# Two-layer decoder trunk on one core: row pools opened amid the gate tiles, seven PSUM banks outside the scores, later spreads and stores, the root on ScalarE

## The chip, the core and the metric

The kernel runs on one core of a Trainium2 chip. TensorE does the matmuls, VectorE (DVE), ScalarE (ACT) and GpSimd (POOL) the elementwise work; each takes its instructions in the order in which they were written to it. SyncE (SP) issues all DMAs, also in order. The metric is the device time of one execution in microseconds; lower is better.

## What is computed

Two post-norm layers on 1024 tokens of width 1024. Layer A mixes with dilated sliding-window attention (three dilations, merged by their softmax denominators), layer B with windowed grouped-query attention with sinks. Cut to what matters here:

```
h = x @ w_in                                   # q, k, v and the gate columns z
o = merged or windowed attention of q, k, v
m = (o * silu(z)) @ w_out                      # output projection
x = layer_norm(ALPHA * x + m, ln_g, ln_b)
x = x + sigmoid(x @ w_gate) * (p @ w_proj)     # the second gate
```

## The kernel before

Every product runs on pairs of f16 numbers (high and low part): `lin` makes one 128x512 tile of a product with 24 matmuls (8 steps of the contraction, three products each). A layer is a chain of such tiles, 8 row tiles of 128 tokens for each block of 512 weight columns. Between the matmuls of a tile `sub_tick` puts attention units (scores, softmax, values) in, so that TensorE has work while they go on.

Weights come as a list of blocks. `weight_steps` is a generator that runs one step of it at a time: load a block by four DMAs, take four maxima on VectorE (`wpm`), put the maximum on a diagonal (`max_diag`, tile `mdd`), spread it over the partitions with one small TensorE matmul into a bank `s` (`max_spread`, `s<-mdd,ones`), make scales, and split each quarter into its high part (ScalarE) and low part (VectorE). `progress` and `prepare` advance it after each tile of a product by a number of steps that is given there.

After the attention of a layer come the gate tiles z (`z_block`, `z_tile`): two halves of 512 columns, 8 row tiles each. ScalarE reads the PSUM tile twice (`zt`, `zu`), VectorE joins them, SP stores them in DRAM (`za`, `zb`). Then `mixed` runs the output projection. `rows(n)` loads the mixed attention (`ot`) and the gate (`og`), multiplies them on GpSimd, takes the row maximum on ScalarE, splits the product (`rhl`) and transposes it by a DMA into `ogT`. `norm(n)` multiplies `ogT[n]` with both halves of the output weights (the blocks `whl` and `wo`), adds the residual `y`, normalises (`rsqrt`) and transposes the result into `xgT`, from which `gate` computes the second gate (blocks `whl` and `wg`). At the end of each layer's attention `drain` runs what is left of units and merges before the pools of the rows are opened. A scheduler of the framework sorts each engine's instructions once more when the program is built, so the order on an engine is not that of the code alone.

PSUM has eight banks: three for `lin`, four for `s`, one for `o`. Before the change all product tiles use the three of `lin`, except in the startup.

Of the kernel before, what the change touches and what calls it, by code (L numbers as in the profile page):

```python
# [20 lines left out]
P = 128  # L21
S = 1024
D = 1024
# [57 lines left out]
W_OP = 2  # L81
N_WAKE = 8
Z_AHEAD = 1
# [5 lines left out]
class Block:  # L89
# [14 lines left out]
    def maxima(self):  # L104
        k, q = self.k, self.n // 4
        pm = k.small.tile([P, 4], F32, tag="wpm", name="wpm")
        for c in range(4):
            k.nc.vector.tensor_reduce(pm[:, c:c + 1], self.raw[:, c * q:(c + 1) * q], axis=AX.X, op=ALU.max,  # L108
                                      apply_absolute_value=True)
            yield True  # L110
        diag = k.max_diag(pm)
        yield True
        e = k.max_spread(diag)
        self.s, self.inv = k.keep(1, "s"), k.keep(1, "inv")
        k.pow2_of(e, self.s, self.inv)
        yield True
# [22 lines left out]
class Trunk:  # L139
    def __init__(self, ctx, tc, a):  # L140
# [13 lines left out]
        self.uid = 0  # L154
# [25 lines left out]
        self.mhalf = self.const.tile([P, 1], F32, name="mhalf")  # L180
        nc.gpsimd.memset(self.mhalf, -0.5)
# [7 lines left out]
    def rope_tables(self, order):  # L189

        t = self.const.tile([P, N_ROPE], F32, name="rope", tag="rope", bufs=2)
# [124 lines left out]
    def drain(self):  # L316
        due, self.due = self.due, []
        for e in due:
            e[1]()
        while self.units or any(self.pipe):  # L320
            self.unit_step()
        self.merge_every = 1
        while self.merges or self.merging:
            self.merge_step()

# [9 lines left out]
    def rope_out(self, ps, nq, nk, n, dst):  # L335
# [6 lines left out]
        t2 = w.tile([P, 512], F32, tag="t2", name="t2")  # L342
# [8 lines left out]
        hl = w.tile([P, 12, P], F16, tag="hl", name="hl", bufs=3)  # L351
# [251 lines left out]
    def next_block(self):  # L603
        b = self.blocks[self.bi]
        self.bi += 1
        while not b.done:
            assert next(self.steps)
        return b
# [13 lines left out]
    def layer_a(self):  # L622
# [14 lines left out]
        for pair in range(2):  # L637
            for g in (1, 2, 0):
                self.rope_tables(g)
# [4 lines left out]
                for n in range(NT):  # L644
                    ps = self.ps_lin.tile([P, 512], F32, tag="lin", name="lin")
                    self.lin(ps, blk, *self.stat_a(g, n), 0, 512)
                    self.v_out(ps.rearrange("p (s c) -> p s c", s=2), vh[:, pick, n, :], vl[:, pick, n, :])
                    self.progress()
# [18 lines left out]
        self.z_block(self.invx, lambda n: self.stat_a(0, n))  # L667
        self.drain()
# [15 lines left out]
    def unit_a(self, q, g, n, qk, vh, vl, cs, ncs, cv, scr):  # L684
# [4 lines left out]
        def stats():  # L689
            st = at.tile([P, 4 * HD + 8], F32, tag="st", name="st", bufs=len(self.pipe) + 1)  # L690
            return st, st[:, 4 * HD:4 * HD + 4], st[:, 4 * HD + 4:]
# [20 lines left out]
    def z_rows(self, pool, ps, c):  # L712
# [4 lines left out]
        u = pool.tile([P, 512], F32, tag="t2", name="zu")  # L717
# [9 lines left out]
    def z_block(self, invx, stat):  # L727

        self.z_stat = stat
        self.upt = 2.0  # L730
        for half in range(2):
            self.w_z = self.next_block()
            self.cz = self.prod(invx, self.w_z.inv, 0.5, "cz")
            for n in range(Z_AHEAD if half else NT):
                self.z_tile(self.work, n, half)
                self.progress()
            if half == 0:
                self.w_z.released = True

    def merge(self, n, pair, scr):  # L740

        nc, at, sp = self.nc, self.att, self.small
# [44 lines left out]
    def layer_b(self, xT, invx):  # L787
# [42 lines left out]
        self.z_block(invx, lambda n: self.stat_t(xT, n))  # L830
        self.drain()
# [45 lines left out]
    def mixed(self, l, xres, gate_pool):  # L877
# [4 lines left out]
        g_b = pw.tile([P, D], F32, tag="g_b", name="g_b", bufs=1)  # L882
        b_b = pw.tile([P, D], F32, tag="b_b", name="b_b", bufs=1)
        nc.sync.dma_start(g_b, a["lng"][l].partition_broadcast(P))
        nc.sync.dma_start(b_b, a["lnb"][l].partition_broadcast(P))
# [3 lines left out]
        w_o, cw = [], []  # L889
# [17 lines left out]
        def norm(n):  # L907
            y = pw.tile([P, D], F32, tag="row", name="y", bufs=6)
            nc.sync.dma_start(y, xres(n))
            sc = sp.tile([P, 2], F32, tag="osc", name="osc")  # L910
            st = sp.tile([P, 2, 6], F32, tag="bst", name="bst")
            for hf in range(2):
                sl = slice(512 * hf, 512 * hf + 512)
                nc.vector.tensor_mul(sc[:, hf:hf + 1], ris[n], cw[hf])
                ps = self.ps_lin.tile([P, 512], F32, tag="lin", name="lin")
# [13 lines left out]

        done = 0  # L930
        for n in range(Z_AHEAD, NT):
            self.z_tile(self.work, n, 1)
            self.tick()
            self.prepare(5)
            if n >= NT - ROWS_AHEAD:
                rows(done)
                done += 1
        self.w_z.released = True
        for i in range(2):
            b = self.next_block()  # L940
            c = self.keep(1, "cw")
            nc.vector.tensor_scalar(c, b.inv, 1.0 / ALPHA, None, op0=ALU.mult)
            w_o.append(b)
            cw.append(c)
        for n in range(NT):
# [4 lines left out]
            if n == 1:  # L950
                wg = gate_pool()
        for b in w_o:
            b.released = True
        return xgT, xg_dr, wg

    def gate(self, l, xgT, xg_dr, last):

        nc, a, pw = self.nc, self.a, self.pw
        w_g = [self.next_block(), self.next_block()]
# [5 lines left out]
        for n in range(NT):  # L965
# [5 lines left out]
            for c0, c1 in ((0, 512), (512, 768), (768, 1024)) if end else ((0, 512), (512, 1024)):  # L971
                hf, sl, w = c0 // 512, slice(c0, c1), c1 - c0
                ps = self.ps_lin.tile([P, 512], F32, tag="lin", name="lin")[:, :w]
                self.lin(ps, w_g[hf], *self.stat_t(xgT, n), c0 % 512, w)
                t = pw.tile([P, 512], F32, tag=("g_b", "b_b")[hf], name="gth", bufs=1)[:, :w]
# [18 lines left out]
    def rsqrt(self, var):  # L994
# [5 lines left out]
        nc.gpsimd.tensor_tensor(r, v, self.mhalf, op=ALU.pow)  # L1000
# [6 lines left out]
    def build(self):  # L1007
# [39 lines left out]
        work, self.work = opened("work", 2)  # L1047
        lower.append(work)
        with tc.tile_pool(name="att", bufs=2) as self.att:
            self.layer_a()  # L1050
        tp, self.tp = opened("tp", 9, side="right")
        pw, self.pw = opened("pw", 2, side="right")

        def gate_pool(name):
# [3 lines left out]
            return p  # L1058

        xgT, xg_dr, wg = self.mixed(0, lambda n: a["x"][n * P:(n + 1) * P, :], lambda: gate_pool("wg"))  # L1060
        x2T, x2_dr = self.gate(0, xgT, xg_dr, False)
        close(wg)
        close(pw)
# [3 lines left out]
        with tc.tile_pool(name="kv", bufs=1) as self.kv, tc.tile_pool(name="att2", bufs=2) as self.att:  # L1067
            self.layer_b(x2T, self.x2_s[1])
        pw, self.pw = opened("pw2", 2, side="right")
        xgT, xg_dr, wg = self.mixed(1, lambda n: x2_dr[n], lambda: gate_pool("wg2"))  # L1070
        self.gate(1, xgT, xg_dr, True)
        close(wg)
        close(pw)
        close(tp)
# [69 lines left out]
```

## Time and profile before

| | us |
|---|---|
| median of 3 runs | 1663.25 (1661.86 to 1665.62) |
| profiled execution, own time | 1667.52 |
| its span on the core | 1665.7 |
| TensorE busy | 1592.0 |
| VectorE busy | 1085.1 |
| ScalarE busy | 923.8 |
| GpSimd busy | 677.8 |

The span is that of the profiled execution; about 2 us lie around it in its own time. TensorE is busy for most of the span, so the time is what TensorE needs, plus what it waits, plus what it loses while its clock is at the lower of its two levels. The mean granted clock was 0.984 of 2.4 GHz.

### The profile page before, as it was taken

What the parts mean: (1) busy time and instruction counts of PE and PEld (TensorE: products, weight loads), DVE (VectorE), ACT (ScalarE), POOL (GpSimd) and SP (SyncE); (2) the same over time, 40 slices, a digit from 0 to 9 for tenths busy, and PEclk for the clock granted to TensorE, in tenths of its full rate; (3) what the DMA queues carried; (4) which work ended last, traced back from release to release, by engine and by line L of the source; (5) the groups of instructions that cost most, each with busy time, mean ns of one, the idle gap of its engine ahead of it and who ended that gap; (6) DMA issues with size and microseconds to landing.
All of it is one profiled execution on the core that took longest, in us unless ns stands there. A gap on an engine that the chain in (4) does not pass through costs nothing. (4 is left out here: it accounts for less than half of the span.)

```text
span 1665.7 us, 29033 instructions
## 1 busy us (share of the span) xinstructions
PE 1592.0 (96%) x10579; PEld 883.1 (53%) x10579; DVE 1085.1 (65%) x2617; ACT 923.8 (55%) x2050; POOL 677.8 (41%) x481
## 2 busy tenths in 40 slices
PE   9899999999999799999999988899999998999998
PEld 3455676654555356666555543344455555544444
DVE  6766655655666876556556667887447998777731
ACT  4536764674765376656657843533334878754321
POOL 0205523432564666244235553453323452225341
PEclk9999999999999899999999999999999999999999
DMA  9618766774787768567648986989975898897963
GB/s 363 246 61 168 166 153 134 161 165 112 159 165 201 215 153 163 130 151 158 155 118 170 191 236 203 335 227 257 252 183 116 156 205 176 192 296 212 257 198 110
DMA packets 543792, 311.02 MB, mean 187 GB/s; under 512 B 473120, under 2 KB 494240, under 8 KB 543392
## 3 DMA queue, kind: packets, MB, share of 16 engines
q1 hardware_dynamic: 543648, 309.16, 75.0%
q8 instruction: 83, 1.36, 0.4%
q14 instruction: 61, 0.50, 0.1%
HBM read 137.78 MB, written 54.92 MB: 116 GB/s over the span
## 5 line engine op out<-in xcount | busy, mean ns | idle before, releaser
L270 PE MATMUL lin<-whl,xhl 128*128 128x512 f16 x1280 | 489.9, 383 | 0.0
L271 PE MATMUL lin<-whl,xhl 128*128 128x512 f16 x1280 | 489.2, 382 | 0.0
L272 PE MATMUL lin<-whl,xhl 128*128 128x512 f16 x1280 | 488.9, 382 | 0.0
L399 POOL TENSOR_TENSOR phl<-sm,phl 128x1024 f16<-128x1024 f32 (+1 forms) x88 | 155.1, 1763 | 234.6 <-ACT phl L397 213.0
L349 POOL TENSOR_TENSOR t<-t,t 128x512 f32<-128x512 f32 (+1 forms) x120 | 153.4, 1278 | 236.9 <-DVE t L348 219.9
L108 DVE TENSOR_REDUCE wpm<-wraw 128x1 f32<-128x1024 f32 (+1 forms) x132 | 157.2, 1198 | 99.3 <-DMA wraw<-in_wa_dram 57.2
L272 PEld LDWEIGHTS <-xhl 128*128 128x128 f16 x1280 | 149.6, 117 | 128.2 <-issue 4.6
L270 PEld LDWEIGHTS <-xhl 128*128 128x128 f16 x1280 | 149.5, 117 | 120.0 <-issue 4.3
L271 PEld LDWEIGHTS <-xhl 128*128 128x128 f16 x1280 | 149.8, 117 | 117.0 <-issue 4.0
L393 ACT ACTIVATE sm<-sm,st,cs 128x128 f32<-128x128 f32 (+1 forms) x384 | 203.6, 532 | 3.3
L356 POOL TENSOR_TENSOR hl<-t,hl 128x512 f16<-128x512 f32 (+1 forms) x120 | 146.0, 1217 | 133.0 <-ACT hl L355 133.0
L387 DVE CUSTOM_DVE_ANT_0 sm<-s,tab 128x256 f32<-128x256 f32 (+1 forms) x512 | 157.3, 359 | 34.0 <-PE s L383 28.9
L132 DVE SCALAR_TENSOR_TENSOR whl<-wraw,s,whl 128x1024 f16<-128x1024 f32 (+1 forms) x116 | 169.2, 1510 | 9.6 <-ACT whl L131 9.5
L355 ACT ACTIVATE hl<-t 128x512 f16<-128x512 f32 (+1 forms) x120 | 72.3, 603 | 121.9 <-POOL t L349 120.1
L345 DVE TENSOR_TENSOR t<-lin,rope 128x512 f32<-128x512 f32 (+1 forms) x120 | 79.0, 658 | 89.3 <-PE lin L272 64.5
L131 ACT ACTIVATE whl<-wraw,s 128x1024 f16<-128x1024 f32 (+1 forms) x116 | 121.8, 1123 | 7.0 <-DVE s L210 7.0
L270 PE MATMUL lin<-whl,x2T 128*128 128x512 f16 (+1 forms) x320 | 114.9, 359 | 0.0
L271 PE MATMUL lin<-whl,x2T 128*128 128x512 f16 (+1 forms) x320 | 114.7, 359 | 0.0
L272 PE MATMUL lin<-whl,x2T 128*128 128x512 f16 (+1 forms) x320 | 114.7, 359 | 0.0
L397 ACT ACTIVATE phl<-sm 128x1024 f16<-128x1024 f32 (+1 forms) x128 | 110.3, 862 | 1.3
L359 ACT ACTIVATE hl<-hl 128x512 f16<-128x512 f16 (+1 forms) x104 | 63.3, 608 | 56.5 <-POOL hl L356 56.2
L383 PE MATMUL s<-qk 128*128 128x128 f16 x1120 | 81.8, 221 | 9.9 <-DMA qk<-hl 9.9
(190 smaller groups left out, 2905.3 us busy)
## 6 DMA issues: line engine op xcount, KB each, us to landing
wraw<-in_wa_dram SPq DMA_DIRECT2D x56, 512.0 KB, 5.6
scr<-st SPq DMA_DIRECT2D x96, 132.0 KB, 2.3
gt<-scr SPq DMA_DIRECT2D x48, 264.0 KB, 3.5
wraw<-in_wav_dram SPq DMA_DIRECT2D x24, 512.0 KB, 6.4
prh<-pro SPq DMA_DIRECT2D x32, 256.0 KB, 4.2
wraw<-in_wg_dram SPq DMA_DIRECT2D x16, 512.0 KB, 8.8
wraw<-in_wb_dram SPq DMA_DIRECT2D x16, 512.0 KB, 6.4
xg<-y SPq DMA_DIRECT2D x16, 512.0 KB, 3.4
```

The costliest lines, as they stand in the source:

```text
L108: k.nc.vector.tensor_reduce(pm[:, c:c + 1], self.raw[:, c * q:(c + 1) * q], axis=AX.X, op=ALU.max, apply_absolute_value=True)
L131: nc.scalar.activation(hl[:, 0, sl], self.raw[:, sl], AF.Copy, scale=self.s)
L132: nc.vector.scalar_tensor_tensor(hl[:, 1, sl], self.raw[:, sl], self.s, hl[:, 0, sl], op0=ALU.mult, op1=ALU.subtract)
L270: mm(ps, xh(kt), wh, start=(kt == 0), stop=False)
L271: mm(ps, xh(kt), wl, start=False, stop=False)
L272: mm(ps, xl(kt), wh, start=False, stop=(kt == NK - 1))
L349: nc.gpsimd.tensor_add(t1[:, :nh * HD], t1[:, :nh * HD], t2[:, :nh * HD])
L356: nc.gpsimd.tensor_sub(hl[:, :nh, HD:P], rv, hl[:, :nh, 0:HD])
L387: nc.vector.tensor_tensor_reduce(sm[:, h, :nk], ps[:, i, :nk], mask, 1.0, -3e38, ALU.add, ALU.max, mx[:, h:h + 1])
L393: nc.scalar.activation(sm[:, h, :nk], sm[:, h, :nk], AF.Exp, bias=nbias[:, h:h + 1], scale=cs, accum_out=sums[:, h:h + 1])
L397: nc.scalar.activation(hl[:, 0], sm[:, :, :nk], AF.Copy)
L399: eng.tensor_sub(hl[:, 1], sm[:, :, :nk], hl[:, 0])
```

## The change

- **Pools.** The pools of the rows (`pw`, `tp`) open as soon as the last attention unit is through, amid the gate tiles of the first half (`gate_tiles`), not after all merges; `drain` is gone. What the merges need (`gt`, `st`) moves to a pool of its own, `attm`, and `hl` to `att`. The pool of the last gate block (`wg`) opens ahead of the output projection, and holds `g_b` and `b_b`, which are loaded there.
- **Banks.** `bank()` takes product tiles from `lin` and `s` in turn, seven banks in all, in the second half of z, the output projection and the second gate.
- **Spreads.** From the first gate tile to the second gate, the spread of a weight block's maximum comes two tiles of TensorE work after its diagonal.
- **Stores and steps.** A gate tile is stored after the next one is written; `zu` has three buffers. The numbers of weight steps change: 3 a tile in both halves of z (before: 1.6 and 5) and 1 a tile in the output projection (before: 2).
- **Root.** The inverse root of the variance is a square root on ScalarE and a reciprocal on VectorE, not a power on GpSimd.
- **Rope.** One buffer instead of two, loaded at the third tile of the block that precedes its use.

```diff
 W_STEPS = 1.6
-W_OP = 2
+SPREAD = 2.0
+W_OP = 1
-Z_AHEAD = 1
+W_GATE = 3
...
         diag = k.max_diag(pm)
         yield True
+        at = k.work_done + SPREAD
+        while k.work_done < at and k.late:
+            yield False
         e = k.max_spread(diag)
...
+    def bank(self):
+        self.turn += 1
+        pool, tag = ((self.ps_s, "s"), (self.ps_lin, "lin"))[self.turn % 7 % 2]
+        return pool.tile([P, 512], F32, tag=tag, name=tag)
...
     def z_tile(self, pool, n, half):
-        ps = self.ps_lin.tile([P, 512], F32, tag="lin", name="lin")
+        ps = self.bank() if half else self.ps_lin.tile([P, 512], F32, tag="lin", name="lin")
         self.lin(ps, self.w_z, *self.z_stat(n), 0, 512)
-        self.nc.sync.dma_start(self.z_dr[n][:, 512 * half:512 * half + 512], self.z_rows(pool, ps, self.cz))
+        out = self.z_out
+        self.z_out = (self.z_dr[n][:, 512 * half:512 * half + 512], self.z_rows(pool, ps, self.cz))
+        for o in (out, self.z_out if half and n == NT - 1 else None):
+            if o:
+                self.nc.sync.dma_start(*o)
...
+    def gate_tiles(self, leave):
+        self.upt = 2.0
+        self.late = True
+        self.z_block(0)
+        for n in range(NT):
+            self.z_tile(self.work, n, 0)
+            self.progress(W_GATE)
+            if leave and not (self.due or self.units or any(self.pipe)):
+                leave()
+                leave = None
...
+        self.z_block(1)
         done = 0
-        for n in range(Z_AHEAD, NT):
+        for n in range(NT):
             self.z_tile(self.work, n, 1)
             self.tick()
-            self.prepare(5)
+            self.prepare(W_GATE)
             if n >= NT - ROWS_AHEAD:
                 rows(done)
                 done += 1
+        while self.merges or self.merging:
+            self.merge_step()
+        gp = gate_pool()
+        g_b = gp.tile([P, D], F32, tag="g_b", name="g_b", bufs=1)
+        b_b = gp.tile([P, D], F32, tag="b_b", name="b_b", bufs=1)
...
         for n in range(NT):
             norm(n)
...
-            if n == 1:
-                wg = gate_pool()
...
         r = sp.tile([P, 1], F32, tag="rr", name="rr")
-        nc.gpsimd.tensor_tensor(r, v, self.mhalf, op=ALU.pow)
+        nc.scalar.activation(r, v, AF.Sqrt)
+        nc.vector.reciprocal(r, r)
```

The first place is TensorE where the gate tiles of layer A end (`xhl` is the layer's input, `ogT` the transposed row of the output projection). Before:

```order
L271 MATMUL lin<-whl,xhl 128x512
L272 LDWEIGHTS xhl
L272 MATMUL lin<-whl,xhl 128x512
L235 LDWEIGHTS ones
L235 MATMUL s<-mdd,ones 128x128
L270 LDWEIGHTS ogT
L270 MATMUL lin<-whl,ogT 128x512
```

In the changed kernel there:

```order
L275 MATMUL lin<-whl,xhl 128x512
L276 LDWEIGHTS xhl
L276 MATMUL lin<-whl,xhl 128x512
L274 LDWEIGHTS ogT
L274 MATMUL s<-whl,ogT 128x512
```

The spread between the last gate tile and the first tile of the output projection is gone, and that tile goes to a bank of `s`. After the last value matmul of the attention both kernels have 10 gate tiles to go. Before, four spreads stand behind 1, 5, 7 and 10 of them; in the changed kernel the first two stand behind 0 and 8, the third behind the fourth tile of the output projection, and the fourth between its last tile and the first tile of the second gate.

The second place is SP's queue ahead of the first rows in layer A (`za_609`, `oa_601` and so on are row tiles in DRAM, numbered on by one; `lng`, `lnb` the weights of the normalisation). Before:

```order
L725 DMA za_611<-zu 128x512
L884 DMA g_b<-in_lng_dram 128x1024
L885 DMA b_b<-in_lnb_dram 128x1024
L894 DMA ot<-oa_601 128x1024
L895 DMA og<-za_609 128x1024
L894 DMA ot<-oa_602 128x1024
L895 DMA og<-za_610 128x1024
```

In the changed kernel (row tile 0 is `za_610` and `oa_602` here):

```order
L731 DMA za_610<-zu 128x512
L103 DMA wraw<-in_wg_dram 128x1024 x2
L905 DMA og<-za_610 128x1024
L904 DMA ot<-oa_603 128x1024
L731 DMA za_611<-zu 128x512
L782 DMA oa_608<-gt 128x2x256
L782 DMA oa_609<-gt 128x2x256
L731 DMA za_612<-zu 128x512
L905 DMA og<-za_611 128x1024
L904 DMA ot<-oa_604 128x1024
L905 DMA og<-za_612 128x1024
```

The first row's loads move ahead of the last two merges' stores; those of the second and third row stay behind them and behind the store of the third gate tile. `g_b` and `b_b` move down, behind the loads of the last weight block.

The third place is VectorE, layer A, ahead of the low parts of the second half of the output weights (`wo`; `m<-s` reads what the spread made). Before:

```order
L237 TENSOR_REDUCE m_11746<-s 128x1
L766 TENSOR_TENSOR gt<-gt 128x2x256
L719 SCALAR_TENSOR_TENSOR zu<-zt,zu 128x512
L216 TENSOR_REDUCE m_11833<-wpm 128x1
L209 TENSOR_SCALAR inv_11749<-m_11746 128x1
L224 TENSOR_SCALAR mdt<-m_11833 128x1
L210 RECIPROCAL s_11748<-inv_11749 128x1
L942 TENSOR_SCALAR cw_12028<-inv_11749 128x1
L226 TENSOR_SCALAR mde<-mdt 128x1
L228 TENSOR_SCALAR mdd<-tab,mde 128x128
L132 SCALAR_TENSOR_TENSOR wo<-wraw,s_11748,wo 128x1024 x4
```

In the changed kernel, from the third row on (`p2t<-rm` is the first step on a row's maximum):

```order
L205 TENSOR_SCALAR p2t<-rm 128x1
L207 TENSOR_SCALAR p2e<-p2t 128x1
L213 TENSOR_SCALAR ri<-p2e 128x1
L214 RECIPROCAL rs<-ri 128x1
L241 TENSOR_REDUCE m_11857<-s 128x1
L213 TENSOR_SCALAR inv_11860<-m_11857 128x1
L214 RECIPROCAL s_11859<-inv_11860 128x1
L954 TENSOR_SCALAR cw_11580<-inv_11860 128x1
L266 SCALAR_TENSOR_TENSOR rhl<-og,rs,rhl 128x1024
L921 TENSOR_SCALAR osc<-cw_11580,ri 128x2 x2
L721 SCALAR_TENSOR_TENSOR zu<-zt,zu 128x512
L136 SCALAR_TENSOR_TENSOR wo<-wraw,s_11859,wo 128x1024 x4
```

The scale of `wo` now stands behind the maxima of three rows, where before no row stood ahead of it. ScalarE has four more table loads: in each layer one ahead of the first row's square root and one behind the last, ahead of the second gate's first tanh.

## Rows read from the trace of the kernel before

**Rows 1.** The page, busy time: engine, us, share of the span, instructions.

```profile
PE 1592.0 (96%) x10579; PEld 883.1 (53%) x10579; DVE 1085.1 (65%) x2617; ACT 923.8 (55%) x2050; POOL 677.8 (41%) x481
```

**Rows 2.** What TensorE waited for: us in total, times, longest us.

```profile
PE s L235 <- DVE mdd L228: 21.9, 4, 7.4
PE s L383 <- DMA qk<-hl: 9.9, 6, 4.0
PE o L414 <- ACT st L694: 8.7, 4, 4.9
PE o L414 <- DVE mu L858: 8.7, 6, 2.7
PE o L414 <- DMA pT<-phl: 8.6, 5, 4.7
```

**Rows 3.** Timeline of TensorE, layer A: start, us, instruction, [idle before it].

```profile
992.59 0.19 PE L416 MATMUL o<-vh,pT 128*128 128x64 f16 x1
...
995.21 0.38 PE L270 MATMUL lin<-whl,xhl 128*128 128x512 f16 x1
...
995.86 0.38 PE L270 MATMUL lin<-whl,xhl 128*128 128x512 f16 x1
...
1035.32 0.29 PE L235 MATMUL s<-mdd,ones 128*128 128x128 bf16 x1 [6.17 <-DVE mdd L228]
...
1061.33 0.29 PE L235 MATMUL s<-mdd,ones 128*128 128x128 bf16 x1 [7.44 <-DVE mdd L228]
...
1061.89 0.59 PE L270 MATMUL lin<-whl,ogT 128*128 128x512 f16 x1 [0.27 <-PE s L235]
...
1118.68 0.39 PE L270 MATMUL lin<-whl,ogT 128*128 128x512 f16 x1 [2.94 <-DMA ogT<-rhl]
...
1154.47 0.38 PE L270 MATMUL lin<-whl,xgT 128*128 128x512 f16 x1
```

**Rows 4.** The same for layer B, where its gate tiles end.

```profile
1492.71 0.29 PE L235 MATMUL s<-mdd,ones 128*128 128x128 bf16 x1 [3.32 <-DVE mdd L228]
```

**Rows 5.** Windows: stretch, length, busy us of PE, PEld, DVE, ACT, POOL, clock, DMA.

```profile
1060.00:1065.00 5.00, 3.40 (x9) 1.26 (x10) 4.51 (x12) 4.44 (x6) 0.00 (x0) 0.51 0.99 225
1061.90:1154.50 92.60, 86.85 (x387) 38.30 (x388) 77.39 (x159) 32.32 (x36) 42.26 (x24) 0.97 0.95 254
1492.80:1578.50 85.70, 85.70 (x386) 38.37 (x387) 65.05 (x122) 32.10 (x35) 39.13 (x22) 0.97 0.90 238
```

**Rows 6.** Timeline of VectorE, ScalarE and SP, layer A, weights and first row.

```profile
1019.28 1.53 SPq L102 DMA_DIRECT2D wraw<-in_wg_dram  x2
...
1024.69 1.22 DVE L108 TENSOR_REDUCE wpm<-wraw 128x1 f32<-128x1024 f32 x1 [1.55 <-DMA wraw<-in_wg_dram]
...
1034.53 0.33 SPq L725 DMA_DIRECT2D za<-zu  x1
...
1034.98 0.29 DVE L228 TENSOR_SCALAR mdd<-tab,mde 128x128 bf16<-128x128 f32 x1
...
1036.33 4.26 ACT L131 ACTIVATE wo<-wraw,s 128x1024 f16<-128x1024 f32 x4 [9.02 <-DMA oa<-gt]
...
1037.57 1.01 SPq L895 DMA_DIRECT2D og<-za  x1
...
1048.90 0.15 DVE L201 TENSOR_SCALAR p2t<-rm 128x1 f32<-128x1 f32 x1 [4.61 <-ACT ot L900]
...
1052.55 4.89 SPq L874 DMA_TRANSPOSE ogT<-rhl  x1
```

**Rows 7.** Tile ogT, 1036 to 1170: from issue to landing.

```profile
DMA to landing us min/median/max: 4.3/4.7/7.5
```

**Rows 8.** VectorE, layer A, the evacuation of the output projection.

```profile
1126.09 1.41 DVE L917 SCALAR_TENSOR_TENSOR y<-lin,osc,y 128x512 f32<-128x512 f32 x2 [4.00 <-DMA y<-in_x_dram]
```

**Rows 9.** Groups: busy us, mean ns, idle before: the root, the table load, low parts.

```profile
L1000 POOL TENSOR_TENSOR rr<-rv,mhalf 128x1 f32<-128x1 f32 x16 | 22.5, 1403 | 61.7 <-DVE rv L998 50.9 <-DMA wraw<-in_wb_dram 7.8 <-DVE rs L210 3.1
...
L486 ACT ACT_TABLE_LOAD x1 | 1.3, 1283 | 0.7 <-PEq L1133 0.7
...
L132 DVE SCALAR_TENSOR_TENSOR whl<-wraw,s,whl 128x1024 f16<-128x1024 f32 (+1 forms) x116 | 169.2, 1510 | 9.6 <-ACT whl L131 9.5
```

More of the change, by code (lines that the diff above doesn't have):

```diff
@@ L153, in __init__ @@
         self.o_i = 0
-        self.uid = 0
+        self.uid = self.turn = 0
+        self.z_out = None
+        self.late = False
         self.bufs = 2
@@ L189, in rope_tables @@
     def rope_tables(self, order):
-        t = self.const.tile([P, N_ROPE], F32, name="rope", tag="rope", bufs=2)
+        t = self.const.tile([P, N_ROPE], F32, name="rope", tag="rope")
         self.nc.sync.dma_start(t, self.a["tab"][:, order * N_ROPE:(order + 1) * N_ROPE])
@@ L913, in norm @@
                 sl = slice(512 * hf, 512 * hf + 512)
-                nc.vector.tensor_mul(sc[:, hf:hf + 1], ris[n], cw[hf])
-                ps = self.ps_lin.tile([P, 512], F32, tag="lin", name="lin")
+                ps = self.bank()
                 self.lin(ps, w_o[hf], *self.stat_t(ogT, n), 0, 512)
@@ L949, in mixed, with gate @@
                 done += 1
-            if n == 1:
-                wg = gate_pool()
         for b in w_o:
             b.released = True
-        return xgT, xg_dr, wg
-    def gate(self, l, xgT, xg_dr, last):
+        return xgT, xg_dr, gp
+    def gate(self, l, xgT, xg_dr, gp, last):
         nc, a, pw = self.nc, self.a, self.pw
+        self.late = False
         w_g = [self.next_block(), self.next_block()]
@@ L972, in gate @@
                 hf, sl, w = c0 // 512, slice(c0, c1), c1 - c0
-                ps = self.ps_lin.tile([P, 512], F32, tag="lin", name="lin")[:, :w]
+                ps = self.bank()[:, :w]
                 self.lin(ps, w_g[hf], *self.stat_t(xgT, n), c0 % 512, w)
-                t = pw.tile([P, 512], F32, tag=("g_b", "b_b")[hf], name="gth", bufs=1)[:, :w]
+                t = gp.tile([P, 512], F32, tag=("g_b", "b_b")[hf], name="gth", bufs=1)[:, :w]
                 nc.scalar.activation(t, ps, AF.Tanh, scale=cg[hf])
@@ L1046, in build, with row_pools @@
         lower = [xpool]
[L1047 to L1052, printed above, removed]
+        for name in ("work", "attm"):
+            p, pool = opened(name, 2)
+            setattr(self, name, pool)
+            lower.append(p)
+        att, self.att = opened("att", 2)
+        self.layer_a()
+        pools = []
+        def row_pools(first, last):
+            for p in first:
+                close(p)
+            for name, bufs in last:
+                p, pool = opened(name, bufs, side="right")
+                setattr(self, name[:2], pool)
+                pools.append(p)
         def gate_pool(name):
@@ L1057, in gate_pool @@
             p, self.wg = opened(name, 1)
[L1058 to L1063, printed above, removed]
+            pools.append(p)
+            return self.wg
+        self.gate_tiles(lambda: row_pools([att], [("tp", 9), ("pw", 2)]))
+        xgT, xg_dr, gp = self.mixed(0, lambda n: a["x"][n * P:(n + 1) * P, :], lambda: gate_pool("wg"))
+        x2T, x2_dr = self.gate(0, xgT, xg_dr, gp, False)
+        close(pools.pop())
+        close(pools.pop())
         self.pw = self.wg = None
@@ L1066, in build @@
         lower.append(work)
[L1067 to L1074, printed above, removed]
+        kv, self.kv = opened("kv", 1)
+        att, self.att = opened("att2", 2)
+        self.layer_b(x2T, self.x2_s[1])
+        self.gate_tiles(lambda: row_pools([att, kv], [("pw2", 2)]))
+        xgT, xg_dr, gp = self.mixed(1, lambda n: x2_dr[n], lambda: gate_pool("wg2"))
+        self.gate(1, xgT, xg_dr, gp, True)
+        while pools:
+            close(pools.pop())
 @with_exitstack
```

63 lines of the change are left out of this document (24 added, 39 removed).

## The prediction

> **What bounds the kernel.** I read busy times first. TensorE is busy 1592.0 of 1665.7 us [rows 1], so the time is its work, plus 73.7 us in which it stands, plus what a low clock costs. Next I read what it stands for [rows 2]. The largest entry, 21.9 us in four waits, is a small matmul that waits for `mdd`: the spread of a weight block's maximum. TensorE takes its matmuls in order, so while VectorE has not finished that diagonal, the product tiles queued behind it wait too. The others are shared by attention: operands that arrive late (9.9 and 8.6 us), and the bank `o`, which ScalarE or VectorE empties late (8.7 each).
>
> Then I asked where those waits lie [rows 3, 4]. Two spreads at the end of layer A's gate tiles wait 6.17 and 7.44 us, one in layer B 3.32. The remainder of the 21.9, 5.0, is in the startup, which stays as it is. To price a stage I compare its length with its matmuls at the high clock. Three matmuls start 0.65 us apart [rows 3], so a tile of 24 takes 5.2 us.
>
> - *Gate tiles of layer A, after the last value matmul*: from 992.6 to 1061.9, 69.3 us for 10 tiles that need 52.0. Lost: **17.3**. Of these 13.9 are idle (6.17 + 7.44 + 0.27). The other 3.4 are clock: behind the second wait the granted clock is 0.51 of 2.4 GHz, its lower level [rows 5].
> - *Output projection of layer A*: 92.6 us for 16 tiles that need 83.2. Lost: **9.4**, of them 5.7 idle (92.60 less 86.85 busy [rows 5]), the rest clock. The longest of these waits is 2.94 us for a transposed row `ogT` [rows 3].
> - *Layer B*: the wait of **3.3** [rows 4], and in the output projection 85.7 us for 83.2. TensorE never stands there [rows 5], so the **2.5** are clock that the wait left behind.
>
> Together 32.5 us. That is what the change can reach; the waits in attention lie ahead of the first row whose place it moves by more than a few positions.
>
> **The change part by part.**
>
> *Spreads.* They leave the place between gate tiles and output projection. All four of layer A and those of layer B still run, 0.29 us each, so only the waiting goes. What is late next? The second spread of layer A now stands behind 8 gate tiles, which TensorE has done at 992.6 + 8 x 5.2 = 1034.2. Its diagonal was ready at 1034.98 + 0.29 = 1035.3 [rows 6], and what sets that is unchanged: VectorE stands in its queue at a maximum, for a weight load [rows 6]. So a wait of 1.1 us stays. The lower bound is 0, since VectorE has fewer steps ahead of that diagonal than before. The upper is about 4: the first row's two loads now go out next to that weight load, whose first quarter took 1024.69 - 1019.28 = 5.4 us; if they slow it by half, 2.7 come on top. I take 2.
>
> *Pools, and the first row.* Before, the load of `og` went out at 1037.57, `p2t` began at 1048.90 (11.3 us later), the transpose was issued at 1052.55 and needs 4.7 more [rows 6, 7]: from load to `ogT` some 19.7 us. Now the load stands right behind the four weight quarters, whose last was issued at about 1020.8 [rows 6]. Its `p2t` could start at 1032, but on VectorE it stands behind the diagonal (1035.3), so `ogT` is there at 1035.3 + 3.65 + 4.7 = 1043.7. TensorE ends its gate tiles at 1035.3 + 10.4 = 1045.7. No wait, with 2 us to spare; if the load is 2 us slower than before, it is on the path. I add 1 for this and for a clock drop (in layer B a wait of 3.3 was followed by 2.5 of it). The first stage keeps 2 + 1 = **3.0** of its 17.3.
>
> *`wo`, later.* The second spread's result is now read on VectorE behind the third row's maximum, which needs that row's `og`. This load stands behind the third gate tile's store (issued at 1034.53 [rows 6]) and two further loads, so about 1036.5; plus 11.3 is 1047.8; four row steps and the scale, 1048.6. One quarter of the split costs ScalarE 4.26 / 4 = 1.07 [rows 6] and VectorE about 1.5 [rows 9]: the first quarter of `wo` is there at 1051.2. TensorE wants it 5.2 us after 1045.7, at 1050.9. A wait of 0.3, and each next quarter keeps pace with six matmuls (1.3 us). Bounds: 0, and about 5 if that row loads 4 us later. I take **1.5**.
>
> *The rest of the output projection.* What binds a row is the chain load, GpSimd, ScalarE, VectorE, SP. VectorE is busy 77.4 of 92.6 us there [rows 5], and it stands 4.00 us for a residual load with other rows' splits behind it [rows 8]. The weight steps per tile halve, but two splits and two sets of maxima still fall into this stage, so I expect the same 77 in some 88 us. For it: in layer B 65.0 of 85.7 us let TensorE run through [rows 5]. Four rows are prepared before the first `norm`. Seven banks let TensorE run ahead of a late evacuation. Against it: none of these shortens the chain for rows 4 to 7. Lower bound 0 as in layer B, upper the present 9.4. I take **3.0**.
>
> *Root.* 16 powers of 1.40 us on GpSimd go [rows 9]; in their place a one-column ScalarE step and a reciprocal. This shortens a row's normalisation by about 1 us, which the rows above contain. Four table loads of 1.28 us each come in [rows 9]; ScalarE is busy 32.3 of 92.6 us there [rows 5], so I cost them at 0, at most 4 x 1.28 = 5.1 if each lands on the path.
>
> The Trainium skill ("ScalarE: Activation LUTs", What ACT_TABLE_LOAD costs) speaks against this edit: a switch costs about 2.66 us with its drain, and functions should be batched by set. By that the bound would be 10.6 us and the sum, if all of it were on the path, about 1650. The one table load of the trace shows 1.28 and no drain beside it; the rule to batch is kept by the order in which the eight roots of a layer stand between two loads.
>
> *Layer B* has no merges, its attention outputs are stored directly, and `g_b` and `b_b` no longer go out ahead of the rows. Its spread for `wo` stands two tiles ahead of the end, 10.4 us plus 5.2 before `wo` is wanted; the split needs 4 x 1.5. I leave **1.0** of 5.8.
>
> *At no cost:* gate stores one tile later, the third `zu` buffer, `hl` and `gt` in other pools, and the single rope buffer, loaded many tiles before its use. Product tiles between hide them; without that cover a rope load would cost one landing, some 4 us, in each of six phases.
>
> Sum: left are 3.0 + 1.5 + 3.0 + 1.0 = 8.5 of 32.5, a gain of 24.0. The profiled execution took 1667.5, so it would take 1643.5. It lies 4.3 above the median of 1663.25; the same gain from the median gives **1639**.
>
> **Rivals.**
>
> - *Rows are the bound.* TensorE then reaches the output projection earlier and stands for `ogT` and `wo`. For it: the third row's loads move by only about 4 us, VectorE is 84% busy. Against it: the first row moves by 17. If the output projection of layer A still loses its 9.4, `wo` costs 5 more and layer B keeps 3, then with the 3.0 of the gate tiles 20.4 are left, a gain of 12: 1651.
> - *Everything fits.* The output projection of layer A runs like that of layer B, and no spread waits: nearly all 32.5 come back, and some of the waits in attention: 1628.
> - *Weights too late: slower.* The last block's spread now stands at the end of the output projection, its split (`wg`) after it, and the second gate wants `wg` 36 matmuls (7.8 us) later. Between lie VectorE's and ScalarE's backlog and 1.3 us a quarter. If `wg` and `wo` are late in both layers, there are four new waits, each followed by about 2.5 of clock. They use up the gain of 24 when a wait is 3.5 us (4 x (3.5 + 2.5)) beyond my 8.5; at 6 us each it is 4 x 8.5 - 24 = 10 slower, 1673. For it: half as many steps a tile. Against it: ScalarE is idle two thirds of this stage, and in layer B the same splits fit.
> - *Nothing moves.* The waits are exchanged for equal ones: 1663. For it speaks only that the weight load that VectorE waits for is the same.
>
> **How the numbers follow.** Forecast 0.60 (1631 to 1646), rows the bound 0.17 (1646 to 1657), everything fits 0.10 (1622 to 1631), nothing moves 0.05, weights too late 0.08. The predicted time is that of the likeliest, 1639. For 8 in 10 the range takes in the forecast and the two beside it nearly whole: 1625 to 1656. Faster by over 0.2% (about 3.3 us; less can't be told from no change in this kernel) are the first three but for the edge of the second: 0.86; the same 0.05; slower 0.09.
>
> **What would show it.** Right: no wait for `mdd` over 3 us outside the startup; the first `ogT` matmul of layer A some 59 us after the last value matmul (now 69.3); the output projection of layer A at 86 to 89 us, that of layer B at 83 to 84; the clock near full between gate tiles and second gate. Wrong on `wo` or `wg`: TensorE rows that wait for a split at L136. Wrong on rows: waits for `ogT` over 6 us in all. It would be wrong altogether if weight splits are late in both layers, or if the moved loads slow the scores ahead of the gate tiles.

## The result and the profile after

The changed kernel takes 1675.93 us (median of 4 runs, 1673.85 to 1677.35) against 1663.97 for the kernel before on the same chip: ratio 1.0076, 95% interval 1.0062 to 1.0090. It is 12 us **slower**; the forecast was 1639, and all runs lie above its range. The profiled execution took 1676.58 us, with a span of 1674.8. The page's busy times, which answer to [rows 1], say at once that TensorE's work is the same:

```profile
PE 1591.5 (95%) x10579; PEld 883.1 (53%) x10579; DVE 1087.6 (65%) x2617; ACT 930.8 (56%) x2070; POOL 651.0 (39%) x464
```

What TensorE waited for in the changed kernel (us in total, times, longest), to be held against [rows 2]:

```profile
PE lin L274 <- DMA ogT<-rhl: 18.0, 4, 10.6
...
PE s L274 <- DMA ogT<-rhl: 5.2, 2, 4.5
PE s L239 <- DVE mdd L232: 5.0, 1, 5.0
PE s L239 <- DVE mdt L228: 3.8, 1, 3.8
PE lin L274 <- DVE t L348: 3.1, 1, 3.1
PE lin L274 <- ACT wg L135: 2.4, 2, 1.9
```

The waits of spreads at the gate tiles are gone, as forecast; the 5.0 for `mdd` are the startup's. One spread in the gate stage of layer A still waits 3.8 us for its diagonal: the list names an earlier step, `mdt`, but the diagonal itself ends at 1182.71 + 0.28 = 1182.99 and the spread starts at 1183.05. Besides, the list has 23.2 us for transposed rows `ogT` (4.6 in the kernel before), and waits for `t` and `wg` that the kernel before did not have. The timeline of TensorE shows where; the rows without a wait are the last value matmul of layer A (990.30) and the first matmuls of stages. The last row is the diagonal of that spread, on VectorE:

```profile
990.30 0.19 PE L416 MATMUL o<-vh,pT 128*128 128x64 f16 x1
...
1046.88 0.38 PE L274 MATMUL s<-whl,ogT 128*128 128x512 f16 x1 [4.48 <-DMA ogT<-rhl]
...
1113.06 0.61 PE L274 MATMUL lin<-whl,ogT 128*128 128x512 f16 x1 [10.60 <-DMA ogT<-rhl]
...
1147.09 0.38 PE L274 MATMUL s<-whl,xgT 128*128 128x512 f16 x1
...
1183.05 0.23 PE L239 MATMUL s<-mdd,ones 128*128 128x128 bf16 x1 [3.83 <-DVE mdt L228]
...
1236.39 0.27 PE L274 MATMUL lin<-whl,x2T 128*128 128x256 f16 x1
...
1252.79 0.37 PE L274 MATMUL lin<-whl,x2T 128*128 128x256 f16 x1 [3.08 <-DVE t L348]
...
1281.15 1.06 PE L383 MATMUL s<-bk,bq 128*128 128x128 f16 x16
...
1540.81 0.61 PE L274 MATMUL lin<-whl,ogT 128*128 128x512 f16 x1 [5.83 <-DMA ogT<-rhl]
...
1585.36 0.38 PE L274 MATMUL s<-whl,xgT 128*128 128x512 f16 x1
...
1182.71 0.28 DVE L232 TENSOR_SCALAR mdd<-tab,mde 128x128 bf16<-128x128 f32 x1
```

In the kernel before, beside [rows 3, 4], the same starts of gate stage's end, first score and last stage are these:

```profile
1237.69 0.27 PE L270 MATMUL lin<-whl,x2T 128*128 128x256 f16 x1
...
1278.60 1.05 PE L383 MATMUL s<-bk,bq 128*128 128x128 f16 x16 [0.73 <-DMA bq<-hl]
...
1578.45 0.38 PE L270 MATMUL lin<-whl,xgT 128*128 128x512 f16 x1
```

From such starts the span divides into stretches (us). The forecast's column holds the prediction's terms on top of the matmuls; the two right columns are experiments told below. The pause is the change's two tiles of TensorE work between a diagonal and its spread (`SPREAD`).

| stretch | before | forecast | changed | no pause | no pause, `hl` moved back |
|---|---|---|---|---|---|
| start to last value matmul of layer A | 992.6 | 992.6 | 990.3 | 990.6 | 994.0 |
| gate tiles A, to first `ogT` | 69.3 | 55.0 | 56.6 | 54.9 | 54.8 |
| output projection A, to first `xgT` | 92.6 | 87.7 | 100.2 | 94.9 | 94.5 |
| gate stage A, to first `x2T` | 83.2 | 83.2 | 89.3 | 83.0 | 83.0 |
| key tiles B, to first score | 40.9 | 40.9 | 44.8 | 45.1 | 40.3 |
| layer B, to first `xgT` | 299.9 | 295.1 | 304.2 | 300.7 | 296.4 |
| gate stage B, to the end | 87.2 | 87.2 | 89.4 | 87.3 | 87.3 |

The gate tiles of layer A give 12.7 of the 14.3 us that were asked of them. Every stretch after them is longer: 7.6 + 6.1 + 3.9 + 4.3 + 2.2 = 24.1. Less the 12.7, and the 2.3 of the table's first row, that is the 9.1 by which the span grew. The windows of the first two of them (length, busy us of PE, PEld, DVE, ACT, POOL, clock, DMA share), beside [rows 5]:

```profile
1046.90:1147.10 100.20, 88.06 (x387) 38.58 (x388) 76.61 (x158) 40.57 (x51) 30.29 (x16) 0.91 0.93 255
1147.10:1236.40 89.30, 85.02 (x389) 38.02 (x388) 50.85 (x78) 34.00 (x40) 24.88 (x17) 0.98 0.92 232
```

VectorE does the 77 us of work that I expected in the output projection, but in 100 us instead of 88; TensorE stands 12.1 us, and its mean granted clock is 0.91 of 2.4 GHz. What is late there is read from all engines (weights first, then the row that TensorE waits for at 1113.06):

```profile
1020.11 0.81 SPq L103 DMA_DIRECT2D wraw<-in_wg_dram  x2
...
1031.82 0.22 PE L239 MATMUL s<-mdd,ones 128*128 128x128 bf16 x1
...
1035.62 0.29 DVE L232 TENSOR_SCALAR mdd<-tab,mde 128x128 bf16<-128x128 f32 x1
...
1047.77 0.27 DVE L241 TENSOR_REDUCE m<-s 128x1 f32<-128x128 f32 x1
...
1050.12 4.26 ACT L135 ACTIVATE wo<-wraw,s 128x1024 f16<-128x1024 f32 x4
...
1058.37 2.00 SPq L103 DMA_DIRECT2D wraw<-in_wg_dram  x4
...
1064.22 9.00 SPq L888 DMA_TRANSPOSE ogT<-rhl  x1
...
1065.89 1.28 ACT L1015 ACT_TABLE_LOAD   x1
...
1069.84 0.22 PE L239 MATMUL s<-mdd,ones 128*128 128x128 bf16 x1
...
1085.67 0.28 DVE L241 TENSOR_REDUCE m<-s 128x1 f32<-128x128 f32 x1
...
1088.23 4.27 ACT L135 ACTIVATE whl<-wraw,s 128x1024 f16<-128x1024 f32 x4 [2.37 <-DVE ri L213]
1092.40 0.19 ACT L1015 ACTIVATE rr<-rv 128x1 f32<-128x1 f32 x1
...
1099.61 1.15 ACT L935 ACTIVATE y<-y,rr 128x1024 f32<-128x1024 f32 x1 [0.36 <-DVE rr L1020]
...
1103.72 1.15 ACT L265 ACTIVATE rhl<-y,lns 128x1024 f16<-128x1024 f32 x1 [2.87 <-POOL y L936]
1104.78 1.13 ACT L265 ACTIVATE rhl<-og,rs 128x1024 f16<-128x1024 f32 x1
...
1108.08 2.60 SPq L888 DMA_TRANSPOSE ogT<-rhl  x1
```

Read backwards: the sixth row's `ogT` is transposed at 1108.08, because its split on ScalarE (1104.78) stands in the queue behind the normalised second row (1099.61 and 1103.72), whose root (1092.40) stands behind the split of a gate weight (1088.23). That weight, the first half of the second gate, was not loaded late: its load began at 1020.11, and its diagonal was ready at 1035.62 + 0.29 = 1035.9. But its spread stands on TensorE at 1069.84, 34 us later, behind the fourth tile of the output projection, and VectorE reads the result at 1085.67. The spread at 1031.82, read at 1047.77, is that of the block before, `wo`, whose own diagonal was ready long before, at 978.6. The load at 1058.37 is that of the second half of the gate weights (`wg`); it goes out when the split of `wo` is through (1058.1).

### The profile page after: what moved, and what is told of

Read it like the earlier page. It is cut to its first block, busy times and chain, and to the rows that moved or that the text cites. A ratio compares the mean times of both kernels' runs of the same rounds, so it can differ in the third digit from the quotient of the medians.

```text
span 1674.8 us, 29027 instructions
## 1 busy us (share of the span) xinstructions
PE 1591.5 (95%) x10579; PEld 883.1 (53%) x10579; DVE 1087.6 (65%) x2617; ACT 930.8 (56%) x2070; POOL 651.0 (39%) x464
## 5 line engine op out<-in xcount | busy, mean ns | idle before, releaser
L274 PE MATMUL lin<-whl,xhl 128*128 128x512 f16 x1248 | 475.7, 381 | 0.0
L276 PE MATMUL lin<-whl,xhl 128*128 128x512 f16 x1248 | 475.5, 381 | 0.0
L275 PE MATMUL lin<-whl,xhl 128*128 128x512 f16 x1248 | 475.3, 381 | 0.0
L274 PE MATMUL lin<-whl,x2T 128*128 128x512 f16 (+1 forms) x280 | 100.5, 359 | 3.1 <-DVE t L348 3.1
L275 PE MATMUL lin<-whl,x2T 128*128 128x512 f16 (+1 forms) x280 | 100.4, 359 | 0.0
L276 PE MATMUL lin<-whl,x2T 128*128 128x512 f16 (+1 forms) x280 | 100.4, 358 | 0.0
L383 PE MATMUL s<-qk 128*128 128x128 f16 x1120 | 82.0, 221 | 10.6 <-DMA qk<-hl 10.6
```

What stands on the lines that cost most here:

```text
L274: mm(ps, xh(kt), wh, start=(kt == 0), stop=False)
L275: mm(ps, xh(kt), wl, start=False, stop=False)
L276: mm(ps, xl(kt), wh, start=False, stop=(kt == NK - 1))
```

## Experiments

First the parts one by one, and the load of `g_b` and `b_b`.

**Root back on GpSimd**

```
+        self.mhalf = self.const.tile([P, 1], F32, name="mhalf")
...
-        nc.scalar.activation(r, v, AF.Sqrt)
-        nc.vector.reciprocal(r, r)
+        nc.gpsimd.tensor_tensor(r, v, self.mhalf, op=ALU.pow)
```

> The changed kernel with the root back on GpSimd (power -0.5), so no root and no table load on ScalarE. Theory R (the root stands in ScalarE's queue ahead of the splits of rows 4 and 5, which waited there 17 us after their scale was ready): the wait of 10.6 us for the sixth row's ogT in layer A falls below 4 and that of 5.8 in layer B too; total some 10 us less than the changed kernel, about 1666. Rival L (the loads of g_b and b_b, 10.6 us to land, stand among the rows' loads) and rival W (weight work put off by one step a tile): the waits stay, the total stays within 3 us of 1676.

1683.69 us, ratio 1.0113 (1.0093 to 1.0133) to the kernel before, as all ratios below. The wait for the sixth row stays at 10.2 and the gate stage of layer A waits 5.9 for a weight. Theory R falls: the root is not what holds ScalarE up. The total is 7.8 us above the changed kernel, where L and W had it unchanged: with the pause, the root on ScalarE is a gain.

**Two weight steps a product tile**: `W_OP = 1` to `W_OP = 2`.

> The changed kernel with two weight steps a tile in the output projection, as before. Theory W (one step a tile puts the spreads of the gate stage and the split for layer B off): the wait of 3.8 us for a maximum's spread in the gate stage of layer A, the 3.1 at the start of layer B and the 1.9 for a weight in the last stage go, with the clock they cost: some 8 to 10 us less, about 1667. Theories R and L: the waits for ogT in the two output projections stay (10.6 and 5.8), total 1672 or more; more weight work ahead of the rows may lengthen them.

1687.70 us, 1.0142 (1.0127 to 1.0157). Half of theory W holds: the gate stage of layer A goes back to 83.0. But the output projection grows to 118.7, with waits for `ogT` of 7.7, 9.2 and 8.8. It seems that late weight work costs there or in the gate stage, and that this edit only chooses where. The wait at the start of layer B stays (2.9), so it does not hang on this pace.

**Three banks instead of seven**

```
-        pool, tag = ((self.ps_s, "s"), (self.ps_lin, "lin"))[self.turn % 7 % 2]
+        pool, tag = self.ps_lin, "lin"
```

> The changed kernel with three banks in place of seven for the second half of the gate tiles, the output projection and the gate stage. If seven banks only let the matmuls run ahead of late evacuations, which VectorE must then do later in a row: within 3 us of 1676. If they bring a gain that hides part of the loss: TensorE waits for a bank (VectorE y, ScalarE gate) and the total is 5 us or more above 1676.

1680.37 us, 1.0098 (1.0072 to 1.0123). Between the two: the waits turn into others (for `y` 2.0 and 1.9, for `ogT` 4.2, for `wg` 4.3), and the interval overlaps that of the changed kernel.

**No loads of `g_b` and `b_b`**: the two `dma_start` lines give way to `memset`.

> The changed kernel without the two loads of g_b and b_b in either layer: they are set to 1 and 0 by GpSimd, so the normalised rows lack their weight and offset. Theory L: the transposition of the fourth row no longer takes 9.0 us to issue, the next row's loads go out some 7 us earlier, the 10.6 us wait falls below 4, and the total is 8 to 12 us less, about 1666. Theory R or W: the load of og comes earlier, but the split of rows 4 and 5 still stands behind root and row on ScalarE; the wait stays above 7 and the total within 4 us of 1676.

The normalised rows lack their weight and offset here. 1677.24 us, 1.0081 (1.0059 to 1.0103). Theory L falls: the fourth row's transposition still takes 8.7 us to issue, and the sixth row is waited for 13.2.

**Five weight steps a gate tile**: `W_GATE = 3` to `5`. **No pause**: `SPREAD = 2.0` to `0.0`.

> The changed kernel with five weight steps behind each gate tile, as before, instead of three. Theory W (fewer steps in the gate tiles push the load, maximum and split of the weights for the gate stage among the rows, and the later ones into the gate stage): the output projection of layer A falls from 100 to 94 or less, the wait in the gate stage (3.8) and at the start of layer B (3.1) shrink, total 1668 or less. Theory C (the rows are a loop: the split of row n+4 stands on ScalarE behind the normalised row n, and both share two buffers): the wait for ogT of about 10 us stays, total within 3 us of 1676 or above it.

> The changed kernel with SPREAD = 0, so a spread is issued one step behind its diagonal, as before. If the later spreads are what moved the waits on: less delay for the weights, the waits for weights in both gate stages go and the total is 1668 or less. If they do what I forecast: waits for mdd of 3 us and more come back at the gate tiles, total 1676 to 1685. Theory C: the waits for ogT stay.

Five steps: 1663.18 us, 0.9999 (0.9990 to 1.0008). No pause: 1660.71 us, 0.9988 (0.9975 to 1.0001). Either takes back the loss, 13 and 15 us. Five steps, in both halves of the gate tiles, do it with the pause in place, and at a price: the first row is waited for 15.6 us (gate tiles 67.7), and only the later stretches are short (89.1 and 83.0). Without the pause the gate tiles keep their 54.9. The timeline of this second kernel, the same weights as above:

```profile
1021.75 0.22 PE L239 MATMUL s<-mdd,ones 128*128 128x128 bf16 x1
...
1034.36 0.29 DVE L232 TENSOR_SCALAR mdd<-tab,mde 128x128 bf16<-128x128 f32 x1
...
1034.81 0.28 DVE L241 TENSOR_REDUCE m<-s 128x1 f32<-128x128 f32 x1
...
1036.44 4.25 ACT L135 ACTIVATE wo<-wraw,s 128x1024 f16<-128x1024 f32 x4
...
1037.35 0.22 PE L239 MATMUL s<-mdd,ones 128*128 128x128 bf16 x1
...
1045.77 1.94 SPq L103 DMA_DIRECT2D wraw<-in_wg_dram  x4
...
1058.95 4.26 ACT L135 ACTIVATE whl<-wraw,s 128x1024 f16<-128x1024 f32 x4 [1.73 <-DVE s L214]
```

On TensorE the spread of `wo` comes 10.1 us earlier, the next one, that of the gate weight's first half, 32.5 us, though its diagonal is ready only 1.3 us earlier. The read of the first spread and the split of `wo` come 13.0 and 13.7 us earlier, the load of `wg` 12.6, the split of the gate weight's first half 29.3, ahead of the late rows. The windows of its output projection and gate stage:

```profile
1045.60:1140.50 94.90, 86.77 (x386) 38.04 (x387) 80.98 (x152) 39.60 (x50) 27.66 (x16) 0.97 0.96 270
1140.50:1223.50 83.00, 83.00 (x388) 37.66 (x387) 49.12 (x82) 32.03 (x39) 28.34 (x18) 1.00 0.94 242
```

TensorE's waits that are not for rows or in attention (us in total, times, longest):

```profile
PE s L239 <- DVE mdd L232: 5.0, 1, 5.0
PE lin L274 <- DVE t L348: 3.2, 1, 3.2
```

The gate stage runs at full clock without a wait. And the waits for `mdd` do not come back, against what I expected: three steps a gate tile alone put the spreads behind their diagonals. The margin is small; the spread at 1037.35 starts 2.7 us after its diagonal.

**A buffer each for the splits of the two kinds of row** (`tag="rhl"`, two, becomes `"rho"` and `"rhl"`, one each), and **five rows ahead** (`ROWS_AHEAD = 5`).

> The changed kernel with a buffer of its own for the split of the attention rows (one) and one for the split of the normalised rows, in place of two that both take in turn. Theory C, if the shared buffers make the loop: the fifth and sixth rows' splits no longer wait for normalised rows, the 10.6 us wait falls below 4, total 1668 or less. If ScalarE's order alone makes it, or with one buffer each the transpositions of neighbouring rows can't overlap: the same or slower, 1676 to 1690. Theory W: no change, 1673 to 1679.

> The changed kernel with five rows prepared ahead of the first product of the output projection instead of four. Theory C: the loop is one row (10.4 us) longer, so that row n+5 waits for the normalised row n; the wait of 10.6 us for a row in layer A and of 5.8 in layer B fall below 4, total 1666 or less. Theory W: five rows need more of VectorE and ScalarE ahead of the weights, waits for wo or wg instead; total 1673 or more.

1682.37 us, 1.0118 (1.0099 to 1.0137), with a wait of 15.8 for `ogT`; and 1678.30 us, 1.0089 (1.0074 to 1.0104). Nothing here speaks for the shared buffers as the cause, but the run can't rule them out: with one buffer for each kind neighbouring rows of a kind may wait for each other, and so cost what the separation brings. With five rows the output projection falls to 92.5, but the gate stage grows to 96.7 with waits for `y` (3.7) and `wg` (4.4): rows that go ahead of the weights push these back.

**The pause alone, in the kernel before**

```
+        at = k.work_done + SPREAD
+        while k.work_done < at and k.late:
+            yield False
         e = k.max_spread(diag)
...
+        self.late = True
...
+        self.late = False
```

> The kernel before with nothing but the pause put in: from the gate tiles to the end of the output projection, two tiles of matmuls between a weight block's diagonal and its spread. Theory P (the pause is taken in the one sequence of steps for all blocks, so every block puts off the load, maxima and split of all that follow): the waits for mdd at the gate tiles go, the load of the gate weights comes 10 us or more later, among the rows, and the total is not lower but 5 to 20 us higher than before, 1668 to 1683. Rival Q (the pause harms only with three steps a gate tile and one in the output projection; with five and two there is room): the 13.6 us of waits in layer A go and the total is 1650 to 1663.

1677.54 us, 1.0090 (1.0072 to 1.0108): the pause by itself costs 15 us there too, as P says, but elsewhere than I wrote, and the waits for `mdd` do not go. What this kernel waited for:

```profile
PE s L240 <- DVE mdd L233: 22.2, 2, 17.2
PE lin L275 <- DMA ogT<-rhl: 12.7, 2, 9.2
```

In layer A one wait for `mdd` of 17.2 takes the place of the two of 13.6, with no loss before the gate stage. The loss lies in layer B: its first row is waited for 9.2 (from the last value matmul to it 34.7 us instead of 27.6), and its output projection takes 92.2 instead of 85.7.

**A kept step**: a step that falls into the pause is made up for (`yield None` in the pause, and `prepare` gives its credit back).

> The changed kernel with its pause of two tiles, but a step that falls into the pause is kept and made up for behind it, where the changed kernel drops it together with the tile's other steps. Theory S (the loss is the dropped steps, three a gate tile and one a product tile): the split of the second block of wo falls back from 1050 to 1042 or earlier, the waits for ogT fall to 5 or less, total 1660 to 1668. Theory D (the delay of two tiles for each block in a row is enough): total within 4 us of 1676.

1683.15 us, 1.0125 (1.0103 to 1.0148), 7 above the changed kernel: neither theory's total. The split of the gate weight's first half comes at 1070.33 instead of 1088.23, that of `wo` only at 1047.47 instead of 1050.12, not at the 1042 that S asked for. So the steps that the pause drops are not simply the loss: made up for later, they come among the rows (output projection 108.5, with waits of 7.7 and 8.7 for `ogT`; gate stage 83.0). A gate weight that is split 18 us earlier does not help there, so its lateness alone is not the price; where the weight work falls among the rows counts as well.

**`hl` of layer B in `work2`**, without the pause and with it

```
-        hl = self.att.tile([P, 12, P], F16, tag="hl", name="hl", bufs=3)
+        hl = self.hl_pool.tile([P, 12, P], F16, tag="hl", name="hl", bufs=3)
...
         work, self.work = opened("work2", 2)
+        self.hl_pool = self.work
```

> The changed kernel without the pause (SPREAD = 0), and with the buffers hl of layer B's rope in the pool work2, as before, instead of att2. Theory H (in att2 they lie where the split of the last x2T row lay, so the first key tiles wait for its transposition, and TensorE for their banks): the wait of 3.1 to 3.3 us for t at the start of layer B goes, the stretch from the first x2T matmul to the first score falls from 45 to 41, total 1656 to 1658. Rival (the wait comes from the late weight block there): stretch and total as without the pause alone, 1660 to 1661.

> The changed kernel, pause and all, with hl of layer B in the pool work2. If the price of hl's place is one of its own: 4 to 9 us less than the changed kernel, 1667 to 1672, the wait for t at the start of layer B gone. If it was one only without the pause: within 3 us of 1676.

Without the pause 1652.51 us, 0.9942 (0.9926 to 0.9957): 8 us less than with `hl` in `att2`, and **faster than both kernels**, by 10 us than the kernel before. With the pause 1672.64 us, 1.0060 (1.0045 to 1.0075), 3 less than the changed kernel, with intervals that overlap; it lies between the two things expected. In both the key tiles fall from 45 to 40 and the wait for `t` goes. ScalarE in the kernel without the pause, `hl` still in `att2`, shows what held them:

```profile
1238.55 0.51 ACT L355 ACTIVATE hl<-t 128x128 f16<-128x128 f32 x2 [4.13 <-DMA x2T<-rhl]
```

The first write of `hl` waits for the transposition of the last `x2T` row, of which it needs nothing: theory H holds for that wait. The key tiles account for 4.8 of the 8 us. The stretch behind them falls too (300.7 to 296.4), but that is not shown to come from `hl`: with the pause the same move leaves it at 304.2 and 304.3, and its part from the first score to the last value matmul ranged from 184.4 to 188.9 in the five kernels that have `hl` moved back and no pause.

**On top of this: five rows ahead, five steps a gate tile, root on GpSimd, three banks**

> The same with five rows prepared ahead instead of four. Theory C in what is left (row n+4 stands behind the normalised row n: five waits for ogT of 1 to 3 us in layer A's output projection): they fall below 2 in all, total 3 to 6 us less than with four, 1651 to 1654. If the rows are bound by VectorE and ScalarE in all: no change, or up to 3 more.

> The same with four rows, and with five weight steps behind each gate tile instead of three. Theory P: the pause was the loss, so that five steps add nothing now: within 3 us of the run with three, 1655 to 1660. If three steps a tile are a loss by themselves: 4 us or more below it. If they hold up the first row, as with the pause (15.6 us for the first ogT): 5 us or more above it.

> Without the pause, hl in work2, and the root back on GpSimd. If the root on ScalarE shortens each row's normalisation, as the 7.8 us with the pause say: 4 to 9 us above 1652.5, in the output projections and the gate stages. If, as I forecast, root and table loads cost and bring nothing in the total: within 3 us of it, 1650 to 1656.

> Without the pause, hl in work2, and three banks in place of seven. If the seven banks keep TensorE running over late evacuations: waits for y and for the gate's activations of 1 to 4 us come back in the output projections, 4 us or more above 1652.5. If they bring nothing where nothing is late: 1650 to 1656.

Five rows: 1653.33 us, 0.9943 (0.9928 to 0.9958), no change: the output projection of layer A falls from 94.5 to 86.9, its gate stage rises from 83.0 to 90.0. Five steps: 1655.49 us, 0.9949 (0.9933 to 0.9965), within the 3 us of P; a wait for `mdd` of 12.2 is back. Root on GpSimd: 1653.82 us, 0.9944 (0.9924 to 0.9964), no change. Three banks: 1661.45 us, 0.9990 (0.9979 to 1.0002), 9 us more. TensorE waits for evacuations that seven banks cover:

```profile
PE lin L274 <- DVE y L927: 11.3, 7, 2.7
...
PE lin L274 <- ACT zu L720: 5.8, 3, 3.0
```

Not all of these waits are loss. The output projection of layer A, with most of those for `y`, takes 94.3 against 94.5, as the waits for `ogT` there are gone in turn; the gate tiles of layer A (59.9 instead of 54.8) and the output projection of layer B (87.3 instead of 84.4) are longer.

## Why the prediction was wrong

**The step that failed** is the one on the spreads: "All four of layer A and those of layer B still run, 0.29 us each, so only the waiting goes". I read the pause as a change of place of one matmul on TensorE and put its delay of the weights at nothing. But the steps of all weight blocks are one sequence, and while it stands for two tiles, everything behind that spread in it stands too: scales, split, the next load and its maxima. The delay grows from block to block: 10.1 us for the spread of `wo`, 32.5 for the next, and the split of the gate weight comes 29.3 us later, among the rows. Five steps a gate tile make it up; three, with one a product tile, do not. Taking the pause out gives 15 us back; putting it into the kernel before costs 15.

The term for the spreads also rests on a wrong pairing. The diagonal of 1035.3 that I gave to layer A's second spread belongs to the third, whose maxima are those that wait for `in_wg` there [rows 6]; the second's, that of `wo`, is ready at 978.6 in both kernels. So the wait of 1.1, taken as 2, could not come, and the third spread, which moved into the output projection, has no term in the sum.

**The rest of the output projection** was mis-sized: I left 3.0 (and 1.5 for `wo`), measured are 100.2 - 83.2 = 17.0. `wo` itself came as forecast and is waited for only 0.39 us (at 1055.81). VectorE's work there is the 77 us that I expected, but the split of the next weight came later, ahead of the rows in VectorE's and ScalarE's queues, and the rows then came late. **Layer B**: I left 1.0 of 5.8; the stretch to its first `xgT` takes 9.1 more than forecast. Its wait for `mdd` of 3.3 is gone, but its output projection takes 92.9 instead of 85.7, with a wait of 5.8 for `ogT`. Without the pause this falls to 84.6, while the first row is then waited for 4.3; together 3.5 us go. The stretch then takes 300.7, still not less than the 299.9 before; why stays open.

**"At no cost … `hl` and `gt` in other pools"** failed for `hl` in layer B: 3.1 us of wait, and 0.8 of clock (granted 0.96 in the key tiles, 1.00 before). I named the cover (product tiles), but not that a new place can have another owner, who is late.

**What held.** No spread waits at the gate tiles of layer A; though three steps, not the pause, are why. That this stage takes 56.6 against 55.0 forecast is in part luck: of the 3.0 that I left, 2 were for a spread that did not wait, and 1 for the first row, which is waited for 4.5. Its transposition went out at 1039.52, nearly as forecast (1039.0), but took 7.2 us to land and not 4.7. The root at no cost: without the pause, 1653.82 against 1652.51; with it, the root on ScalarE even gains 7.8. The Trainium skill ("ScalarE: Activation LUTs", What ACT_TABLE_LOAD costs) has about 2.66 us for a switch with its drain; the 10.6 that four would cost by it, an estimate, are not seen in the time here. The loads took 1.28 us each. Of seven banks I wrote that they let TensorE run ahead, and gave it no number: it is 9 us without the pause; with it 4, with intervals that overlap.

**The rivals.** "Weights too late", 0.08, had the sign and nearly the time (1673), but by four waits for weights. Those are 0.4, 0.5 and 1.9 us, and 3.8 for a spread; the greater part was paid in rows, as "rows are the bound" would have it. Neither rival saw that the first causes the second. The test that I set for rows (over 6 us for `ogT`) was met with 23.2.

**Open.** Which of load, maxima and split of a late weight delays the rows most was not taken apart; the way from the late split to the late row is read from one trace, and the kept step shows that it is not the whole account. Nor is it known why the output projection of layer A does not fall below 94.5 with four rows ahead and three steps, where 83.2 are needed.

## What to carry to other kernels

When an edit delays one step, ask what sequence that step belongs to, and price everything behind it on every engine, not only the matmul that moves. A gain at one stage's start is kept only if the work that had its place beside the old wait still gets done in time; so compare, weight by weight, when load, diagonal, spread and split go out, and take care which diagonal belongs to which spread. And price a buffer's new place by who used that memory last.

## What the runs showed of the hardware

A transposing DMA of one row held SP's queue for 1.78 to 9.00 us in the changed kernel (16 issues of `ogT`), and the loads queued behind it went out that much later. The 9.00 came behind four quarters of a gate weight, a gate tile's store and the loads of `g_b` and `b_b`; without these last two it was 8.67, so they are not the cause. What in the queue makes it long was not isolated.
